# A six-chunk depthwise convolution on TensorE, roots as a power on GpSimd, weight splits on VectorE

## The chip, the cores and the metric

The kernel runs on one core of one Trainium2 chip. The metric is the device time of one execution in microseconds. Of the kernel before there are three timed runs (2513.06 to 2517.64 us, median 2514.32) and one profiled execution.

## The reference, cut to what matters

Two blocks in a row, on 256 tokens of 1024 features. The first block has two layers with a second stream, `ctx`, of 256 tokens beside `x`. Layer 0 of it is a half feed-forward, a conformer convolution and a half feed-forward; layer 1 has attention in the place of the convolution. Each part is preceded by an RMS norm that is scaled and shifted by a projection of a condition vector ("modulation"). The second block has a mixer of two kinds of attention with normed heads (AB), a gated feed-forward, a small gate, and then the same with a compressed and windowed attention (NSA).

```python
def rmsnorm(x, g):
    y = xf * lax.rsqrt(jnp.mean(xf * xf, axis=-1, keepdims=True) + NORM_EPS)
    return y.astype(x.dtype) * g
...
def conformer_conv(h, pw1_w, pw1_b, dw_w, dw_b, ln_g, ln_b, pw2_w, pw2_b):
    a = h @ pw1_w + pw1_b
    u, g = jnp.split(a, 2, axis=-1)
    u = u * jax.nn.sigmoid(g)
    u = lax.conv_general_dilated(u, dw_w[:, None, :], (1,), padding=[(15, 15)], ..., feature_group_count=D_MODEL) + dw_b
    mu = jnp.mean(uf, axis=-1, keepdims=True)
    var = jnp.mean(jnp.square(uf - mu), axis=-1, keepdims=True)
    u = (uf - mu) * lax.rsqrt(var + NORM_EPS) * ln_g + ln_b
    return jax.nn.silu(u) @ pw2_w + pw2_b
```

The depthwise convolution has 31 taps for each of the 1024 channels. Every `rsqrt` in both blocks is over one number per token (or per token and head).

## The kernel before

Features lie on the 128 partitions in eight chunks, tokens in the free dimension, 256 for each stream, so a product for both streams has 512 columns. Each weight product is three TensorE products (lines 337 to 339, or 360 to 362): the fp32 weight is split into a high part `wh` (ScalarE, L306) and a low rest `wl` (L308), in up to four or eight pieces for each loaded tile. `wl` is VectorE's, but in the two mixers of the second block `on_pool` gives the first pieces of a tile to GpSimd (ABP = 4, NSP = 2). Weights come in 1 MB loads on SP's DMA queue (L310), and the reductions of the modulation (L492, from `ada_t`) run on VectorE beside the work of each stage.

The order of the work on each engine is that of the code, in which a small planner, `Flow`, interleaves. It keeps a clock that each product group advances; `put(delay, f)` runs a step when that clock has passed the delay, `fill(gen, period)` draws steps of a generator at a period, and `until` runs steps until a condition holds. So an engine's order is fixed in advance, and each engine works its list in order.

A norm's root: squares are added chunk by chunk (ScalarE squares, GpSimd adds, L386 in `sq_add`), TensorE sums over partitions with a column of ones (L390), VectorE scales (L397) and takes the root in `rsqrt_small`: an integer first guess and three Newton rounds, ten VectorE instructions (L370, L373, L374, L376). Then `spread` puts the column on a diagonal (L406) and TensorE broadcasts it (L407).

The convolution: first the pointwise product for chunk pairs, gate and up, and the gating (L823, L824). Chunks 0 to 3 (`DIRECT`) are convolved tap by tap, 20 taps on VectorE (L841), 11 on ScalarE and GpSimd (L854, L855). Chunks 4 to 7 (`Taps`) go to DRAM (`gated`, L891) and come back with four copies (L897), each shifted by one token, on 32 channels' partitions, so that a 128x32 product (L907) applies four taps to 32 channels at once; its weights are diagonal matrices that GpSimd builds (L880). Each product is for one stream. The results are gathered with a shift by a pivot (L934) and their sums and squares added by GpSimd (L951, L955) for the LayerNorm's mean and variance (L964), then applied (L984, L985, L1040) and given to the second pointwise product, pw2.

The heads in the second block: `head_rms` reduces squares for each head (L1423), scales (L1425), takes the root and multiplies (L1437); TensorE transposes the result (L1463).

## Time and profile before

| | |
|---|---|
| median of three runs | 2514.32 us (2513.06 to 2517.64) |
| the profiled execution | 2520.06 us |
| its span, first to last instruction | 2518.2 us |
| mean granted TensorE clock, of 2.4 GHz | 0.970 |
| busy: TensorE / VectorE / ScalarE / GpSimd | 94% / 70% / 43% / 23% |
| DMA | 371.91 MB, 148 GB/s |

The span lies 1.86 us inside the execution's time. Every row below is from this one execution; times are microseconds from the span's start. "Idle before <- releaser" tells how long an engine had stood before an operation, and which operation on which engine ended that.

### The profile page before, as it was taken

How to read it: one execution, taken by the hardware profiler on the slowest of the kernel's cores; microseconds unless marked ns; L12 is line 12 of the kernel's file. 1: busy time of each engine (PE TensorE's matmuls, PEld its weight loads, DVE VectorE, ACT ScalarE, POOL GpSimd, SP SyncE). 2: the span in 40 equal slices, each digit the busy share in tenths (PEclk: the TensorE clock that was granted, in tenths of full speed). 3: DMA queues.
4: the chain of work that ended last, by engine and by line, in shares of the span. 5: the costliest groups of instructions: out<-in, count | busy, mean ns of one | idle time of the engine just before them, and what ended most of it. 6: DMA issues, size and time to landing. Idle time of an engine off the chain costs nothing. (4 is left out here: it accounts for less than half of the span.)

```text
span 2518.2 us, 40157 instructions
## 1 busy us (share of the span) xinstructions
PE 2360.3 (94%) x15397; PEld 2107.0 (84%) x15397; DVE 1754.9 (70%) x3816; ACT 1075.2 (43%) x2497; POOL 569.3 (23%) x595
## 2 busy tenths in 40 slices
...
GB/s 262 232 158 176 125 176 151 59 126 67 64 138 138 177 104 167 97 138 150 184 150 209 105 68 110 254 205 168 114 103 176 187 177 177 118 66 161 176 176 114
DMA packets 313149, 371.91 MB, mean 148 GB/s; under 512 B 9307, under 2 KB 298236, under 8 KB 305148
## 3 DMA queue, kind: packets, MB, share of 16 engines
...
## 5 line engine op out<-in xcount | busy, mean ns | idle before, releaser
L337 PE MATMUL ps<-a,wh 128*128 128x256 f32 (+2 forms) x4032 | 1310.7, 327 | 20.3 <-ACT wh L306 9.2
L339 PE MATMUL ps<-a,wl 128*128 128x256 f32 (+2 forms) x4032 | 1310.0, 325 | 6.5 <-DVE wl L308 6.5
L338 PE MATMUL ps<-a,wh 128*128 128x256 f32 (+2 forms) x4032 | 1311.7, 326 | 3.7 <-DVE a L1290 1.4
L306 ACT ACTIVATE wh<-stg 128x512 fp32r<-128x512 f32 (+1 forms) x1280 | 609.5, 539 | 598.9 <-PE ps L338 328.5
L337 PEld LDWEIGHTS ps<-a,wh 128*128 128x128 f32 x4032 | 771.3, 192 | 93.1 <-ACT wh L306 11.2
L339 PEld LDWEIGHTS ps<-a,wl 128*128 128x128 f32 x4032 | 774.5, 192 | 68.0 <-DVE wl L308 7.5
L338 PEld LDWEIGHTS ps<-a,wh 128*128 128x128 f32 x4032 | 775.5, 192 | 66.6 <-POOL a L553 2.0
L308 DVE TENSOR_TENSOR wl<-stg,wh 128x512 fp32r<-128x512 f32 (+1 forms) x1206 | 692.7, 626 | 162.9 <-ACT wh L306 157.2
L561 POOL TENSOR_TENSOR a<-t,a 128x256 fp32r<-128x256 f32 (+1 forms) x128 | 136.2, 1066 | 1338.5 <-ACT a L560 1286.5
L492 DVE CUSTOM_DVE_ANT_0 void<-stg,cb,vec 128x1024 f32<-128x1024 f32 x208 | 276.7, 1330 | 41.3 <-DMA stg<-ada_t 37.4
L560 ACT ACTIVATE a<-t 128x256 fp32r<-128x256 f32 (+1 forms) x152 | 76.5, 504 | 254.9 <-DVE t L621 176.3
L657 DVE SCALAR_TENSOR_TENSOR a<-ps,mv,a 128x256 f32<-128x256 f32 x232 | 101.4, 477 | 77.2 <-PE ps L339 77.1
L621 DVE TENSOR_TENSOR t<-t,ps 128x512 f32<-128x512 f32 x66 | 45.4, 687 | 151.6 <-PE ps L339 139.1
L386 POOL TENSOR_TENSOR acc<-acc,t 128x256 f32<-128x256 f32 x98 | 95.7, 977 | 205.0 <-ACT t L385 201.8
L361 PE MATMUL ps<-wl,a 128*128 128x256 f32 x384 | 112.2, 292 | 8.2 <-DVE wl L308 6.9
L360 PE MATMUL ps<-wh,a 128*128 128x256 f32 x384 | 112.7, 294 | 1.7 <-ACT wh L306 1.7
L308 POOL TENSOR_TENSOR wl<-stg,wh 128x512 fp32r<-128x512 f32 (+1 forms) x74 | 93.8, 1296 | 88.7 <-ACT wh L306 88.7
L362 PE MATMUL ps<-wh,a 128*128 128x256 f32 x384 | 111.3, 290 | 0.0
L620 ACT ACTIVATE t<-ps 128x512 f32<-128x512 f32 x66 | 39.0, 590 | 108.2 <-PE ps L339 108.2
L361 PEld LDWEIGHTS ps<-wl,a 128*128 128x128 f32 x384 | 76.7, 200 | 9.7 <-DVE wl L308 7.3
L360 PEld LDWEIGHTS ps<-wh,a 128*128 128x128 f32 x384 | 76.5, 199 | 2.7 <-ACT wh L306 1.9
L841 DVE SCALAR_TENSOR_TENSOR a<-a,vec,a 128x512 f32<-128x512 f32 x76 | 78.3, 1095 | 0.0
(310 smaller groups left out, 1957.0 us busy)
## 6 DMA issues: line engine op xcount, KB each, us to landing
...
```

Source lines behind the costliest of these rows:

```text
L306: nc.scalar.activation(wh[:, k], st[:, k], AF.Copy)
L308: e.tensor_tensor(wl[:, k], st[:, k], wh[:, k].bitcast(F32), ALU.subtract)
L337: nc.tensor.matmul(out, wh[:, k, js], h, start=(k == 0), stop=False)
L338: nc.tensor.matmul(out, wh[:, k, js], l, start=False, stop=False)
L339: nc.tensor.matmul(out, wl[:, k, js], h, start=False, stop=(k == n - 1))
L360: nc.tensor.matmul(out, h[:, ts], wh[:, k, :], start=(k == 0), stop=False)
L361: nc.tensor.matmul(out, h[:, ts], wl[:, k, :], start=False, stop=False)
L362: nc.tensor.matmul(out, l[:, ts], wh[:, k, :], start=False, stop=(k == n - 1))
L386: nc.gpsimd.tensor_tensor(acc, acc, t, ALU.add)
L492: nc.vector.tensor_tensor_reduce(self.void, st[:, i], self.cb[:, s], 1.0, V("ada_b", 72 * layer + v + i), ALU.mult, ALU.add, mv[layer][:, ...
L561: eng.tensor_tensor(l, src, h.bitcast(F32), ALU.subtract)
L657: nc.vector.scalar_tensor_tensor(x[s][:, m, :], o, g, x[s][:, m, :], ALU.mult, ALU.add)
```

## The change

Convolution: `DIRECT` falls from 4 to 2. The 31 taps of chunks 0 and 1 are all VectorE's, and accumulate in PSUM. Chunks 2 to 7 are tap products. For each, the gated chunk is written to DRAM as plain rows, 128 of 2072 bytes, with three zeros ahead of each stream's tokens, and read back by one DMA of 1.06 MB whose access pattern overlaps: 32 rows at a time, each four times, shifted by one. For this the channel order of the first pointwise weights, their bias and the tap weights is permuted on the host. Write and read-back are on ScalarE's DMA queue, at planned delays `OUT` and `BACK`. A tap product takes both streams (512 columns); for the last two chunks it takes one stream at a time. Tap weights are built one chunk at a time in a pool of three buffers that the modulation's broadcast condition (`cb`) and scratch (`void`) use too; `cb` is loaded anew behind the convolution (`sums.spread()`). The pivot comes from chunk 2.

Roots: `rsqrt_small` is one GpSimd `tensor_tensor` with the power -0.5. Two small scalings of `head_rms` go to GpSimd.

Splits: all `wl` are VectorE's; the odd chunks of a modulation are made as the even ones. Of the convolution's apply, the even chunks' splits are VectorE's now.

Sums: the last chunk's square isn't added by GpSimd, but summed by further products of one column.

```diff
-POOL_TAPS = 11
-DIRECT = 4
-SLICE = 3.5
+DIRECT = 2
+SLICE = 2.9
+LAG = 2
 ADA0 = 4.0
 ADA1 = 5.0
+OUT = 1.5
+BACK = 3.5
...
-PIVN = 1
-GQP = 0
-ABP = 4
-NSP = 2
...
+    mhalf = cp.tile([P, 16], F32, name="mhalf")
+    nc.vector.memset(mhalf, -0.5)
...
-            e = eng or (nc.gpsimd if i < share else nc.vector)
+            e = eng or nc.vector
...
     def rsqrt_small(v, out=None):
-        n = v.shape[1]
-        y = tiny()[:, :n]
-        nc.vector.tensor_scalar(y.bitcast(I32), v.bitcast(I32), -0.5, 1597463007.0, ALU.mult, ALU.add)
-        for i in range(3):
-            t = tiny()[:, :n]
-            nc.vector.scalar_tensor_tensor(t, y, -0.5, y, ALU.mult, ALU.mult)
-            nc.vector.tensor_tensor(t, t, v, ALU.mult)
-            z = out if (i == 2 and out is not None) else tiny()[:, :n]
-            nc.vector.scalar_tensor_tensor(z, t, 1.5, y, ALU.add, ALU.mult)
-            y = z
+
+        y = tiny()[:, :v.shape[1]] if out is None else out
+        nc.gpsimd.tensor_tensor(y, v, mhalf[:, :v.shape[1]], ALU.pow)
         return y
...
+    def sq_last(src, scale=1.0):
+
+        t = tmp()[:, :S]
+        nc.scalar.activation(t, src, AF.Square, scale=scale)
+        return t
...
+            for i, part in enumerate(parts):
+                nc.tensor.matmul(p[:, c0 + t:c0 + t + 1], part[:, t * P:(t + 1) * P], ones[:, 0:1],
+                                 start=(i == 0), stop=(i == len(parts) - 1))
...
+        def spread(self):
+
+            self.cb = [np_.tile([P, D], F32, name="w4", bufs=3) for _ in range(2)]
+            for s, t in enumerate(self.cb):
+                nc.sync.dma_start(t, a["cR"][s:s + 1].to_broadcast([P, D]))
+                nc.scalar.activation(t, t, AF.Silu)
+            self.void = np_.tile([P, D], F32, name="w4", bufs=3)
...
-            if c % 2 == 0:
-                nc.scalar.activation(h, t, AF.Identity, bias=sh)
-                nc.vector.scalar_tensor_tensor(l, t, sh, h.bitcast(F32), ALU.add, ALU.subtract)
-            else:
-                nc.scalar.activation(t, t, AF.Identity, bias=sh)
-                nc.scalar.activation(h, t, AF.Copy)
-                nc.gpsimd.tensor_tensor(l, t, h.bitcast(F32), ALU.subtract)
+            nc.scalar.activation(h, t, AF.Identity, bias=sh)
+            nc.vector.scalar_tensor_tensor(l, t, sh, h.bitcast(F32), ALU.add, ALU.subtract)
...
+    gated = tc.dram_tile([DC - DIRECT, 256 * SW + 3], F32, name="gated")
+    ups = [np_.tile([P, 2, SW], F32, name="up", bufs=2) for _ in range(2)]
+    for t in ups:
+        nc.gpsimd.memset(t[:, :, 0:3], 0.0)
+    nc.scalar.dma_start(gated[:, 256 * SW:], ups[0][0:DC - DIRECT, 0, 0:3])
+    npiv = tmp()
+    sums4 = np_.tile([P, 2, 2 * S], F32, name="w4", bufs=3)
...
-        nv = TAPS - POOL_TAPS
-        zs = [tmp().rearrange("p (s n) -> p s n", s=2) for _ in range(2)]
-        for k in range(max(nv, POOL_TAPS)):
-            for j in range(2 if k < nv else 0):
...
+        ds = [bank() for _ in range(2)]
+        for k in range(TAPS):
+            for j in range(2):
+                y, src, wk = two(ds[j]), padded[:, j, :, k:k + S], V("dw_k", j * TAPS + k)
+                if k == 0:
                     nc.vector.tensor_scalar(y, src, wk, None, ALU.mult)
                 else:
-                    for s in both:
-                        nc.vector.scalar_tensor_tensor(y[:, s], src[:, s], wk, convs[s].npiv, ALU.mult, ALU.add)
-            for j in range(2 if k < POOL_TAPS else 0):
-                c, up, z = m + j, padded[m // 2][:, j], zs[j]
-                src, wk = up[:, :, nv + k:nv + k + S], V("dw_k", c * TAPS + nv + k)
-                if k == 0:
-                    nc.gpsimd.tensor_scalar(z, src, wk, V("dw_b", c), ALU.mult, ALU.add)
-                else:
-                    t = tmp().rearrange("p (s n) -> p s n", s=2)
-                    nc.scalar.activation(t, src, AF.Identity, scale=wk)
-                    nc.gpsimd.tensor_tensor(z, z, t, ALU.add)
-            if k % 2 == 1:
-                yield True
+                    nc.vector.scalar_tensor_tensor(y, src, wk, y, ALU.mult, ALU.add)
+            yield True
...
+    def tap_weights(c):
+
+        t = np_.tile([P, 2 * 2 * S], F32, name="w4", bufs=3)
+        tap_w[c] = t.rearrange("p (n k) -> p n k", k=32)
+        for i in range(2):
             v = V("dw_w", 32 * (c - DIRECT) + 16 * i, 16).unsqueeze(2).to_broadcast([P, 16, 32])
-            nc.gpsimd.tensor_tensor(w, v, eye4.unsqueeze(1).to_broadcast([P, 16, 32]), ALU.mult)
-
-    def two_tap_weights(c, t):
-        for i in range(2):
-            tap_weights(c + i, [t[:, 2 * i], t[:, 2 * i + 1]])
-
-    class Taps:
-        def __init__(self, c, u, g):
-            self.c = c
-            up = tmp()
-            glu(c, u, g, up.rearrange("p (s n) -> p s n", s=2))
-            nc.sync.dma_start(gated[c].rearrange("p g n -> g p n"), up)
-            self.src = slot([P, 4, 2, SW])
-            for n in (0, S):
-                nc.gpsimd.memset(self.src[:, :, :, n:n + 3], 0.0)
-            gc = gated[c].rearrange("p g (s n) -> p (g s) n", s=2)
-            for i in range(4):
-                nc.sync.dma_start(self.src[32 * i:32 * i + 32, :, :, 3 - i:3 - i + S]
-                                  .rearrange("p g s n -> p (g s) n"), gc)
-
-        def products(self, s):
-            p = bank()[:, :S]
-            order = (3, 0, 1, 2, 4, 5, 6, 7)
-            for q in order:
-                lo, hi = max(0, 12 - 4 * q), min(S, S + 15 - 4 * q)
-                n = 4 * q - 12
-                for g in range(4):
-                    nc.tensor.matmul(p[32 * g:32 * g + 32, lo:hi], tap_w[self.c][q // 4][:, q % 4 * 4 + g, :],
-                                     self.src[:, g, s, lo + n:hi + n], start=(q == order[0]),
-                                     stop=(q == order[-1]), tile_position=(0, 32 * g))
-                flow.adv(0.5)
-            return p
+            nc.gpsimd.tensor_tensor(tap_w[c][:, 16 * i:16 * i + 16], v, eye4.unsqueeze(1).to_broadcast([P, 16, 32]),
+                                    ALU.mult)
...
+    def bounce(c, u, g):
+
+        up = ups[c % 2]
+        glu(c, u, g, up[:, :, 3:])
+        d = gated[c - DIRECT]
+
+        def back():
+            chunks[c] = slot([P, 4, 2, SW])
+            nc.scalar.dma_start(chunks[c].rearrange("p g s n -> p (g s n)"),
+                                bass.AP(tensor=d.tensor, offset=d.offset, ap=[[8 * SW, 32], [1, 4], [1, 8 * SW]]))
+
+        def out():
+            nc.scalar.dma_start(d[0:256 * SW].rearrange("(p n) -> p n", p=P), up.rearrange("p s n -> p (s n)"))
+            flow.put(BACK, back)
+
+        flow.put(OUT, out)
+
+    def products(c, streams):
+        p = bank()
+        order = (3, 0, 1, 2, 4, 5, 6, 7)
+        ss = slice(streams[0], streams[-1] + 1)
+        flow.until(lambda: c in chunks)
+        for q in order:
+            lo, hi = max(0, 12 - 4 * q), min(S, S + 15 - 4 * q)
+            n = 4 * q - 12
+            for g in range(4):
+                nc.tensor.matmul(two(p)[32 * g:32 * g + 32, ss, lo:hi], tap_w[c][:, 4 * q + g, :],
+                                 chunks[c][:, g, ss, lo + n:hi + n], start=(q == order[0]),
+                                 stop=(q == order[-1]), tile_position=(0, 32 * g))
+            flow.adv(0.43 * len(streams))
+        take(c, p, streams)
...
+        if c == DIRECT:
+            nc.scalar.activation(y, p, AF.Identity, bias=V("dw_b", c))
+            pv = bank()
+            nc.tensor.matmul(pv, ones, y, start=True, stop=True)
+            nc.scalar.activation(npiv, pv, AF.Copy, scale=-1.0 / P)
+            nc.vector.tensor_tensor(y, y, npiv, ALU.add)
+        else:
+            nc.vector.scalar_tensor_tensor(y, p[:, cols], V("dw_b", c), npiv[:, cols], ALU.add, ALU.add)
+        q = tmp()[:, cols]
+        nc.scalar.activation(q, y, AF.Square)
+        if c == DIRECT:
+            held.extend((y, q))
+        elif c == DC - 1:
+            for s in streams:
+                convs[s].last = (y, q)
+        else:
+            for i, new in enumerate((y, q)):
+                nc.gpsimd.tensor_tensor(sums4[:, i, cols], held.pop(0) if held else sums4[:, i, cols], new, ALU.add)
...
-                split(acts[c], t2, nc.gpsimd)
+                split(acts[c], t2, nc.vector if c % 2 == 0 else nc.gpsimd)
...
+                bounce(c, u, g)
+            if c == DIRECT - 1:
+                flow.fill(direct(), SLICE)
+                tap_weights(DIRECT)
+                tap_weights(DIRECT + 1)
+            if c - LAG >= DIRECT:
+                products(c - LAG, both)
+                if c < DC:
+                    tap_weights(c)
     ws = [wtile(pw2[:, i * 256:(i + 1) * 256], DC) for i in range(3)]
     ws.append(prepare(pw2[:, 768:1024], DC, 256, ap))
     flow.until(lambda: ended)
-    for c in (DC - 2, DC - 1):
-        taps(c, 0)
-    flow.until(lambda: len(ended) == DIRECT // 2)
-    taps(DC - 3, 1)
+    products(DC - 2, (0,))
+    products(DC - 1, (0,))
...
-    taps(DC - 2, 1)
-    taps(DC - 1, 1)
+    products(DC - 2, (1,))
+    products(DC - 1, (1,))
...
+    sums.spread()
...
-        nc.vector.tensor_scalar(e[:, 0:2], var, EPS, None, ALU.mult)
+        nc.gpsimd.tensor_scalar(e[:, 0:2], var, EPS, 0.0, ALU.mult, ALU.add)
         nc.vector.tensor_reduce(v, sq.rearrange("p (n d) -> p n d", d=64), AX.X, ALU.add)
         for t in range(2):
-            nc.vector.tensor_scalar(v[:, t * ng:(t + 1) * ng], v[:, t * ng:(t + 1) * ng], 1.0 / HD, e[:, t:t + 1],
+            nc.gpsimd.tensor_scalar(v[:, t * ng:(t + 1) * ng], v[:, t * ng:(t + 1) * ng], 1.0 / HD, e[:, t:t + 1],
                                     ALU.mult, ALU.add)
...
-    on_pool[0] = ABP
...
-    on_pool[0] = NSP
...
+def by_fours(v):
+
+    v = v.reshape(-1, 2, DC, 4, 32).copy()
+    v[:, :, DIRECT:] = v[:, :, DIRECT:].swapaxes(3, 4).reshape(-1, 2, DC - DIRECT, 4, 32)
+    return v.reshape(-1, 2 * D)
...
-    put("eye4", np.tile(np.eye(32), (4, 1)))
+    put("eye4", np.repeat(np.eye(32), 4, 0))
...
-    nc = bacc.Bacc("TRN2", target_bir_lowering=False, num_devices=1, dynamic_dma_scratch_size=2048)
+    nc = bacc.Bacc("TRN2", target_bir_lowering=False, num_devices=1, dynamic_dma_scratch_size=256)
```

VectorE ahead of the first mixer's heads, before. `tn` and `col` are columns of a few numbers, `t` the heads' values; the row with two `tn` inputs is a Newton step.

```order
L1423 TENSOR_REDUCE tn<-t_15310 128x8
L1383 TENSOR_TENSOR col<-col,tn 128x2
L1425 TENSOR_SCALAR tn<-tn 128x4 x2
L370 TENSOR_SCALAR tn<-tn 128x8
L373 SCALAR_TENSOR_TENSOR tn<-tn 128x8
L374 TENSOR_TENSOR tn<-tn 128x8
L376 SCALAR_TENSOR_TENSOR tn<-tn 128x8
...
L1437 TENSOR_TENSOR t_15309<-t_15130,tn 128x256 x2
L1423 TENSOR_REDUCE tn<-t_15338 128x8
```

Ten steps stand between the scaling L1425 and the product L1437: one L370, and L373, L374 and L376 three times. VectorE at the same place, after (L1387 and L1401 are L1423 and L1437 of before):

```order
L1387 TENSOR_REDUCE tn_14898<-t2_14896 128x8
L1347 TENSOR_TENSOR col_14889<-col_14882,tn_14887 128x2
L305 TENSOR_TENSOR wl_14923<-stg_14921,wh_14922 128x512
L1401 TENSOR_TENSOR t2_14895<-t2_14742,tn_14904 128x256 x2
L305 TENSOR_TENSOR wl_14923<-stg_14921,wh_14922 128x512
L1387 TENSOR_REDUCE tn_14911<-t2_14909 128x8
L305 TENSOR_TENSOR wl_14923<-stg_14921,wh_14922 128x512
L1401 TENSOR_TENSOR t2_14908<-t2_14743,tn_14917 128x256 x2
L305 TENSOR_TENSOR wl_14923<-stg_14921,wh_14922 128x512
```

The ten steps have left VectorE's list, and weight pieces (L305) that GpSimd had stand between the heads. GpSimd's list at this place, after; L367 is the power:

```order
L376 TENSOR_TENSOR t_14515<-t_14515,t_14707 128x256
L367 TENSOR_TENSOR col<-tn,mhalf 128x2
L367 TENSOR_TENSOR tn<-tn,mhalf 128x2
L1386 TENSOR_SCALAR tn<-col 128x2
L1389 TENSOR_SCALAR tn<-tn 128x4 x2
L367 TENSOR_TENSOR tn<-tn,mhalf 128x8
```

Where weight pieces stood, GpSimd now has for each head group its two scalings and the root.

GpSimd at the norm ahead of the convolution, after. `acc` is the sum of squares of stream 1, the first power (`col`) its root; `w` are tap weights (L866) and, at L924, the convolution's sums:

```order
L376 TENSOR_TENSOR acc<-acc,t_3096 128x256
L376 TENSOR_TENSOR acc<-acc,t_3100 128x256
L376 TENSOR_TENSOR acc<-acc,t_3104 128x256
L866 TENSOR_TENSOR w_3423<-vec,eye_3145 128x512 x2
L866 TENSOR_TENSOR w_3426<-vec,eye_3145 128x512 x2
L866 TENSOR_TENSOR w_3711<-vec,eye_3145 128x512 x2
L367 TENSOR_TENSOR col<-col,mhalf 128x2
L924 TENSOR_TENSOR w_3156<-a_3143 128x512
```

Six tap-weight pieces stand between the last add of a square and the root of the same stream; before, no tap weights were built until the convolution had begun, and the root was VectorE's.

SP's queue in the convolution, before, in which `stg` are weight loads:

```order
L891 DMA gated<-t_3782 4x32x512
L897 DMA a_3787<-gated 32x8x256 x4
L891 DMA gated<-t_3850 4x32x512
L310 DMA stg<-ffn_wi 128x8x256
L897 DMA a_3855<-gated 32x8x256 x4
```

Write and copies of a chunk stood between weight loads. ScalarE there, after; L833 is a gate's sigmoid, L303 a `wh` piece, L908 and L911 belong to the pivot, L916 squares:

```order
L833 ACTIVATE t_3661<-ps,vec 128x512
L881 DMA gated<-up 128x518
L877 DMA a_3698<-gated 128x1x2072
L908 ACTIVATE a_3143<-ps,vec 128x512
L911 ACTIVATE t_3155<-ps 128x512
L916 ACTIVATE t_3709<-a_3143 128x512
L303 ACTIVATE wh<-stg 128x512
L833 ACTIVATE t_3768<-ps,vec 128x512
L303 ACTIVATE wh<-stg 128x512 x6
L881 DMA gated<-up 128x518
L303 ACTIVATE wh<-stg 128x512
L877 DMA a_3805<-gated 128x1x2072
```

The write and the read-back of a chunk have moved among ScalarE's own work, the read-back behind the write.

## Rows read from the trace of the kernel before

**Rows 1.** Page, part 1: busy us, share of the span, instructions.
```profile
PE 2360.3 (94%) x15397; PEld 2107.0 (84%) x15397; DVE 1754.9 (70%) x3816; ACT 1075.2 (43%) x2497; POOL 569.3 (23%) x595
```

**Rows 2.** TensorE's waits: total us, times, longest.
```profile
PE ps L907 <- DMA a<-gated: 22.3, 2, 21.8
PE ps L407 <- DVE t L406: 19.0, 9, 5.2
PE ps L1463 <- DVE t L1437: 18.3, 3, 16.3
PE ps L964 <- POOL acc L955: 15.2, 2, 15.0
PE ps L390 <- POOL acc L386: 9.7, 5, 3.1
```

**Rows 3.** Stretches: us, busy PE PEld DVE ACT POOL, clock, DMA share, GB/s.
```profile
545.00:614.00 69.00, 27.63 (x357) 17.47 (x349) 55.51 (x76) 22.40 (x43) 49.68 (x43) 0.69 0.49 111
1778.00:1795.00 17.00, 0.67 (x3) 0.45 (x3) 16.22 (x34) 6.16 (x13) 11.48 (x10) 0.63 0.44 142
...
2095.00:2235.00 140.00, 120.32 (x924) 114.31 (x923) 111.95 (x358) 83.07 (x227) 51.32 (x70) 0.93 0.39 114
```

**Rows 4.** Timeline of TensorE in the convolution: start, us, operation, idle before.
```profile
450.02 0.40 PE L337 MATMUL ps<-a,wh 128*128 128x512 f32 x1
450.25 0.40 PE L338 MATMUL ps<-a,wh 128*128 128x512 f32 x1
...
486.57 0.79 PE L337 MATMUL ps<-a,wh 128*128 128x512 f32 x1 [9.17 <-ACT wh L306]
...
494.26 0.79 PE L339 MATMUL ps<-a,wl 128*128 128x512 f32 x1 [6.47 <-DVE wl L308]
...
535.19 10.32 PE L907 MATMUL ps<-a,a 128*32 128x256 f32 x192
...
567.28 5.18 PE L907 MATMUL ps<-a,a 128*32 128x256 f32 x64 [21.77 <-DMA a<-gated]
...
594.93 0.58 PE L964 MATMUL ps<-ones,acc 128*128 128x1 f32 x2 [15.00 <-POOL acc L955]
...
610.86 1.46 PE L407 MATMUL ps<-t,ones 128*128 128x128 f32 x8 [2.24 <-DVE t L406]
613.98 1.01 PE L337 MATMUL ps<-a,wh 128*128 128x256 f32 x3 [1.66 <-ACT a L560]
```

**Rows 5.** VectorE: its direct taps (timeline), and a PSUM operand (page, part 5).
```profile
472.97 19.57 DVE L841 SCALAR_TENSOR_TENSOR a<-a,vec,a 128x512 f32<-128x512 f32 x12
...
500.09 8.03 DVE L841 SCALAR_TENSOR_TENSOR a<-a,vec,a 128x512 f32<-128x512 f32 x12
...
L657 DVE SCALAR_TENSOR_TENSOR a<-ps,mv,a 128x256 f32<-128x256 f32 x232 | 101.4, 477 | 77.2 <-PE ps L339 77.1
```

**Rows 6.** Timeline of SP's queue: a chunk's write and its read-back.
```profile
508.80 0.69 SPq L891 DMA_DIRECT2D gated<-t  x1
514.80 2.59 SPq L897 DMA_DIRECT2D a<-gated  x4
```

**Rows 7.** Timeline: VectorE's modulation and root steps, and GpSimd's pieces.
```profile
424.39 1.75 DVE L492 CUSTOM_DVE_ANT_0 void<-stg,cb,vec 128x1024 f32<-128x1024 f32 x1
...
681.67 0.17 DVE L370 TENSOR_SCALAR tn<-col 128x2 int32<-128x2 int32 x1
...
683.43 0.16 DVE L376 SCALAR_TENSOR_TENSOR col<-tn 128x2 f32<-128x2 f32 x1
...
1786.39 1.19 DVE L376 SCALAR_TENSOR_TENSOR tn<-tn 128x8 f32<-128x8 f32 x1
...
1785.06 8.60 POOL L308 TENSOR_TENSOR wl<-stg,wh 128x512 fp32r<-128x512 f32 x7 [3.08 <-ACT wh L306]
```

**Rows 8.** GpSimd's groups: operation xcount | busy us, mean ns | idle before.
```profile
L1485 POOL TENSOR_SCALAR a<-a,tn 128x128 f32<-128x128 f32 x32 | 11.9, 372 | 47.8 <-DVE tn L1523 26.2 <-DVE tn L1859 17.1 <-ACT a L1144 2.9
...
L951 POOL TENSOR_TENSOR acc<-t,t 128x256 f32<-128x256 f32 x1 | 10.0, 9964 | 0.0
```

166 lines of the change are left out of this document (49 added, 117 removed).

## The prediction

> **What bounds the kernel now.** I read the busy times first, then the list of what TensorE waited for, then the table by stage, then the timeline at the long waits. TensorE is busy for 94% of the span, VectorE for 70% and GpSimd for 23% [rows 1]. So whatever this change gains must come out of the remaining 6% (about 153 us, the sum of all of TensorE's idle stretches), out of the slow clock that follows a long idle stretch, and out of the TensorE work itself, of which the change takes none away and adds some. The waits say where that idle time lies [rows 2]: 22.3 us behind the DMA that brings the gated conv input back, 15.2 us behind GpSimd's adds L955, 19.0 us in nine waits for the spread of a norm's root (L406), 9.7 us in five waits for the sum of squares (L386), 18.3 us behind the scaled heads (L1437). The table by stage gives the clock beside it [rows 3]: between 545 and 614 us TensorE is busy for 27.63 of 69 us and was granted 0.69 of its 2.4 GHz; between 1778 and 1795 us it is busy for 0.67 of 17 at 0.63; between 2095 and 2235 us it idles 19.7 us. So the conv is the largest place, then the attention's first heads, then the roots.
>
> **The conv, 450 to 614 us.** The six weight groups of 512 columns begin at 450.02 us and the second pointwise product begins at 613.98 [rows 4]: 164.0 us. Three kinds of wait lie in it: 9.17 and 6.47 us for weight pieces, because VectorE had twelve taps queued ahead of them; 21.77 us for the read-back; 15.00 us for GpSimd's last sums [rows 4]. The taps ahead of the pieces took 19.57 us for twelve with GpSimd adding beside them, and 8.03 us for twelve without [rows 5]: two engines that halve each other.
>
> After the change I count TensorE's own work, all at the 2.4 GHz level.
> - Six chunks, u and g, 24 products each: 288 at 0.23 us (from 450.02 to 450.25 is one step [rows 4]) make 66.2 us. This is as before.
> - Tap products. Of before, the stretch at 535.19 us holds three chunk-streams (one chunk of one stream, 32 products, two records each: 192 records) in 10.32 us [rows 4], so 3.44 us for one. Now twelve chunk-streams run instead of eight (six chunks by two): 41.3 us. Two streams in one product save instructions, not columns, so I take no gain for it.
> - The pivot (a copy out of PSUM and one product of ones): 1.5 us. The sums of stream 0: 1.5 us. From the last tap product to pw2, the spread and the first apply: 613.98 minus 610.86, 3.1 us [rows 4].
>
> Sum 113.6 us, against 164.0. What could still stand in the way: VectorE's work in that stretch is 62 direct taps at 0.67 [rows 5], 20 us of weight pieces and about 10 us of gates and takes, 71 us of 113. The accumulator of the direct taps moves to PSUM, where an operation of half the width keeps a mean of 0.477 us over the whole span, with GpSimd busy or not (L657 [rows 5]), so the halving should go; if not, the 62 take 101 us and the stretch is VectorE's. GpSimd's work is twelve tap-weight pieces and fourteen adds, at 1.23 us each (seven operations of this size in 8.60 us [rows 7]) to 1.6, 32 to 42 us: no bound. The round trip through DRAM: the write is issued at 508.80 and the read-back could be issued at 514.80 [rows 6], 6.0 us, then some 5 us for the transfer. Five of six round trips have two chunks of other work (21 us and more) to hide in; the last has only the products of chunk 6, about 7 us and what is left of the direct part. I allow 2 us there. The two DMAs now stand on ScalarE's queue, and the read-back waits there for the write to land: behind it ScalarE's next weight pieces are held. The order shows one or two pieces between the two, and the pieces behind are those of a group later. I allow 2 us, bounds 0 and 4 times 6.0 us. Conv: 113.6 + 4 = 117.6, a gain of **46.4 us** (bounds 25 and 52).
>
> **The roots.** A root is now ten VectorE steps, the first at 681.67 and the last at 683.43 us, 1.92 us with its end [rows 7], where nothing disturbs it. With GpSimd on weight pieces (from 1785.06) a step takes 1.19 instead of 0.16 us [rows 7]. After, it is one GpSimd `pow` on 2 to 8 columns. No row shows a pow. The nearest rows are GpSimd's 128x128 scaling at 0.372 us [rows 8] and its 128x512 operation at 1.23 [rows 7]; I take 0.4 us plus the two hand-overs between the engines, 0.6 to 0.8 us in all, because two columns are nearer to the first. For the ends I keep 0.2 (the fixed part of the first) and 1.5.
>
> At the norms: of the 19.0 us for L406, 2.24 lie in the conv [rows 4] and some 2 in the opening; 14.8 us belong to the four norms. I take 1.2 us off each of the seven and 3 us more at the last (5.2 us long because the ten steps stood between other work): 10 us of 14.8. Each of the five waits for L386 loses one GpSimd add, about 1 us: 5 us of 9.7 [rows 2]. About 2 us of slow clock go with them. Against this stands a new wait. The order puts six tap-weight pieces on GpSimd ahead of stream 1's root at the norm in front of the conv. They can start only when the modulation's reductions have left the same buffers. The reduction that the new order has last ended at 426.1 us (424.39 and 1.75 [rows 7]); six pieces of 1.23 us, 7.4 us, bring the root to about 434 us. TensorE will be there at about 430. I put 4 us against it (bounds 0 and 8). Norms: **-13 us** (bounds -20 and -2).
>
> **The first heads, 1754 to 1800 us.** TensorE stands 16.33 us for L1437, since the roots of the heads crawl beside GpSimd's pieces [rows 2, 3, 7]. After, GpSimd has no pieces; VectorE takes them. In the order 16 pieces stand among the four heads' steps: 16 x 0.67 = 11 us (by the undisturbed operation of the same size in [rows 5]), plus the reductions and scalings of four heads, 6 us, plus small steps: 18 us from 1754.7, so done at about 1773. TensorE comes for them at 1778. The gap closes, a 1.7 us gap behind it too, and about 2 us of slow clock. If pow costs 1.5 us the four of them still fit. **-20 us** (bounds -10 and -23).
>
> **The second attention, 2095 to 2235 us.** The same two edits apply, but the waits there are many and small, 19.7 us of idle in all [rows 3], and a part of them for weight pieces. VectorE loses some 25 us of root steps and gets 32 pieces, 20 us: about even, so a piece may still come late. I take 7 us of the 19.7 (bounds 2 and 13).
>
> **The other edits.** The last square goes into the sum by one more product of one column instead of a GpSimd add (counted above). ScalarE and GpSimd no longer make the odd chunks of a modulation; VectorE does it at 0.5 us each, in stretches where TensorE has ten times that queued: nothing, and 1 us per norm if the cover is gone. The reload of cR behind the conv puts a 1 MB load on SP and one ScalarE operation ahead of the first apply; this is inside the 2 us above.
>
> **What the skill says.** The Trainium skill, GPSIMD Engine Reference, section 3.1, holds that "use DVE for elementwise" stays the rule, and section 2.1 that the first call of a freshly loaded GpSimd kernel pays about 6 us more without an instruction of its own. The first part does not decide here, since one operation replaces ten. By the second, if pow needs such a load, the estimate would be 6 us worse, 2434. No row here shows such a load. The order has an extra instruction of no named kind on GpSimd ahead of the first pow, in the opening, where TensorE waits for a root.
>
> **The sum.** 46.4 + 13 + 20 + 7 = 86.4 us. The profiled execution took 2520.06 us, 5.7 more than the median of the three runs, so it would go to 2433.7 and the median, 2514.32, to **2428**.
>
> **Rivals.**
> 1. The forecast, 2405 to 2450: chance 0.60.
> 2. *ScalarE's queue becomes the wait.* In each of the last four round trips ScalarE stands for the landing, 6.0 us [rows 6], and the weight pieces behind it reach TensorE late: 24 us less, and some clock lost again: about 2454. For it: the queue is in order, and weight pieces do stand behind the read-back. Against: ScalarE is busy for 22.40 of the 69 us [rows 3]. Chance 0.15.
> 3. *Pow costs 1.5 to 4 us.* Then the norms gain nothing or lose 10 us and the second attention gains nothing: 2514.3 - 46.4 - 10 + 5 = 2463, up to about 2515 at the far end. Chance 0.12.
> 4. *Slower: pow is the bound.* TensorE waits for a root at 12 places (nine L406, three L1437 [rows 2]). GpSimd's longest simple operation took 9.96 us [rows 8], with nothing in the row to say why. At this price 12 x (9.96 - 1.92) = 96 us come on top, while conv, pieces and adds give 58: 2552. It decides from 58 / 12 + 1.92 = 6.8 us. Against: GpSimd's time grows with columns in every other row. Chance 0.06.
> 5. *More:* the second attention's and the norms' waits go entirely and the conv's allowance is not needed: 52 + 20 + 23 + 15 = 110, 2404 and below. Chance 0.07.
>
> **How the numbers follow.** About 0.2% (5 us) is what a measurement of this kernel can tell from no change. Cases 1, 2 and 5 are faster; of case 3 all but 0.04 (split between same and slower); case 4 is slower. With 0.01 of case 2 as same: faster 0.90, same 0.03, slower 0.07. The range takes the forecast's own 2405 to 2450, rival 2 and the near half of rival 3, and its lower end reaches a little into rival 5: 2402 to 2465.
>
> **What would show it.** Right: no wait for the read-back above 3 us in TensorE's list, pw2's first product at about 565 us in the span, the 16 us wait before the first head's transposes gone, pow under 0.5 us, at least 0.9 of the clock in the conv. A wait of some 4 us for the root of stream 1 ahead of the conv is expected. Wrong: waits for ScalarE's weight pieces in the conv (rival 2), pow in microseconds (3, 4), direct taps still at 1.6 us beside GpSimd (then the conv lasts 30 us longer).

## The result, and the profile after

The changed kernel takes **2457.78 us** (median of 4 runs, 2456.79 to 2461.86) against 2513.69 for the kernel before, measured beside it (median of 4, 2511.81 to 2517.64). The ratio is 0.9779, with a 95% interval of 0.9762 to 0.9796: 56 us faster, inside the range, 30 us above the 2428 of the forecast. The profiled execution took 2457.87 us, with a span of 2456.1.

The busy times and the list of what TensorE waited for, after (columns as in [rows 1, 2]; L404/L405 are L406/L407 of before, L387 is L390, L895 the tap products, L940 the convolution's sums, L1401 is L1437, L1105 a copy out of PSUM):

```profile
PE 2366.3 (96%) x15459; PEld 2100.7 (86%) x15459; DVE 1636.6 (67%) x3527; ACT 1039.4 (42%) x2414; POOL 406.4 (17%) x479
```

```profile
PE ps L405 <- DVE t L404: 13.4, 7, 5.8
...
PE ps L387 <- POOL acc L376: 7.4, 4, 2.5
PE ps L1459 <- DVE a L1105: 6.6, 2, 5.3
...
PE ps L940 <- POOL w L924: 4.0, 1, 4.0
PE ps L1101 <- DVE tn L1840: 3.7, 1, 3.7
PE ps L1101 <- DVE a L1105: 3.6, 2, 3.4
...
PE ps L895 <- DMA a<-gated: 1.4, 1, 1.4
```

Of the five waits of [rows 2], the 22.3 us for the read-back are 1.4, the 15.2 for GpSimd's sums 4.0, the 18.3 for the scaled heads are one wait of 0.7 us far down the list, the 19.0 for a root's spread are 13.4 and the 9.7 for the squares 7.4. All idle time of TensorE fell from 153.3 to 85.2 us. New are 5.3 us behind a copy out of PSUM in the first mixer (L1459 for L1105; 0.8 before) and 3.7 us behind a scaling step of the second attention (L1840). The 3.6 us of L1101 for L1105 stood there before too, at 3.7.

To see where the time went I compare the start of the same TensorE instruction in both traces, the spread of a norm's root (L407 before, L405 after), 17 times in the program. The difference grows like this (us, after minus before):

| up to | start before | start after | difference | gain of the part | forecast |
|---|---|---|---|---|---|
| norm ahead of the conv, stream 1 | 434.92 | 429.95 | -5.0 | norms: 5.0 | norms: 13, all of them |
| conv's root | 610.86 | 568.25 | -42.6 | conv: 37.6 | conv: 46.4 |
| norm behind pw2, stream 1 | 684.64 | 648.32 | -36.3 | **6.3 given back** | nothing |
| cross-attention | 1557.62 | 1511.56 | -46.1 | norms: 9.8 | (in the 13) |
| behind the first mixer | 1896.00 | 1837.50 | -58.5 | 12.4 | 20 |
| end | 2497.82 | 2435.73 | -62.1 | 3.6 | 7 |

The table's sum is 6 us more than the medians differ, since the profiled execution of before (2520.06) lay above its median and the one of after does not. Where these 6 us lie is worked out behind the experiments.

The convolution in stretches, after (columns as in [rows 3]), and its timeline on TensorE:

```profile
445.00:545.00 100.00, 98.67 (x620) 64.94 (x618) 73.04 (x111) 30.60 (x53) 12.84 (x11) 1.00 0.48 164
545.00:571.00 26.00, 18.83 (x216) 11.79 (x216) 7.73 (x19) 4.97 (x9) 10.97 (x11) 0.80 0.25 83
```

```profile
429.95 1.22 PE L405 MATMUL ps<-t,ones 128*128 128x128 f32 x4 [5.77 <-DVE t L404]
...
446.06 0.40 PE L335 MATMUL ps<-a,wh 128*128 128x512 f32 x1
...
545.84 3.58 PE L895 MATMUL ps<-a,w 128*32 128x256 f32 x64 [1.36 <-DMA a<-gated]
553.37 0.59 PE L940 MATMUL ps<-ones,w 128*128 128x1 f32 x2 [3.95 <-POOL w L924]
...
568.25 1.16 PE L405 MATMUL ps<-t,ones 128*128 128x128 f32 x8 [0.80 <-DVE t L404]
571.21 0.73 PE L334 MATMUL ps<-a,wh 128*128 128x256 f32 x4 [1.80 <-ACT a L561]
```

For 100 us TensorE is busy for 98.67 at a granted clock of 1.00: the holes of [rows 4] are gone. From 446.06 to 571.21 the convolution takes 125.2 us where it took 164.0. The last 26 us still hold waits of 1.36, 3.95 and 1.80 us, at a clock of 0.80.

GpSimd's groups for L367, the power, after (line, operation, names, shapes, count; then busy us and mean ns of one):

```profile
L367 POOL TENSOR_TENSOR tn<-tn,mhalf 128x8 f32<-128x8 f32 x14 | 23.0, 1641 | 1.2
L367 POOL TENSOR_TENSOR col<-col,mhalf 128x2 f32<-128x2 f32 x14 | 11.9, 854 | 56.0 <-DVE col L395 56.0
...
L367 POOL TENSOR_TENSOR tn<-tn,mhalf 128x4 f32<-128x4 f32 x1 | 1.0, 1024 | 14.1 <-DVE tn L705 14.1
...
L367 POOL TENSOR_TENSOR tn<-tn,mhalf 128x2 f32<-128x2 f32 x1 | 0.7, 698 | 0.7 <-DVE tn L1344 0.7
L367 POOL TENSOR_TENSOR tn<-tn,mhalf 128x1 f32<-128x1 f32 x1 | 0.6, 562 | 6.8 <-DVE tn L1726 6.8
```

The power costs 0.70 us on two columns in most calls and 1.64 on eight. The prediction had one price for both, 0.4.

### The profile page after: what moved, and what is told of

The parts are those of the page before. It is cut to its first block, busy times and chain, and to the rows that moved or that the text cites. A ratio compares the mean times of both kernels' runs of the same rounds, so it can differ in the third digit from the quotient of the medians.

```text
span 2456.1 us, 39668 instructions
## 1 busy us (share of the span) xinstructions
PE 2366.3 (96%) x15459; PEld 2100.7 (86%) x15459; DVE 1636.6 (67%) x3527; ACT 1039.4 (42%) x2414; POOL 406.4 (17%) x479
## 5 line engine op out<-in xcount | busy, mean ns | idle before, releaser
L303 ACT ACTIVATE wh<-stg 128x512 fp32r<-128x512 f32 (+1 forms) x1280 | 609.1, 539 | 591.0 <-PE ps L335 319.6
L305 DVE TENSOR_TENSOR wl<-stg,wh 128x512 fp32r<-128x512 f32 (+1 forms) x1276 | 719.6, 617 | 170.2 <-ACT wh L303 165.4
L562 POOL TENSOR_TENSOR a<-t,a 128x256 fp32r<-128x256 f32 (+1 forms) x120 | 129.6, 1081 | 1373.2 <-ACT a L561 1256.7
L495 DVE CUSTOM_DVE_ANT_0 w<-stg,w,vec 128x1024 f32<-128x1024 f32 x208 | 274.4, 1319 | 43.4 <-DMA stg<-ada_t 39.5
L376 POOL TENSOR_TENSOR acc<-acc,t 128x256 f32<-128x256 f32 x84 | 82.3, 979 | 212.2 <-ACT t L375 209.4
L357 PEld LDWEIGHTS ps<-wh,a 128*128 128x128 f32 x384 | 75.6, 197 | 2.8 <-ACT wh L303 1.9
L359 PEld LDWEIGHTS ps<-wh,a 128*128 128x128 f32 x384 | 75.4, 196 | 0.0
L553 ACT ACTIVATE a<-t,mv 128x256 fp32r<-128x256 f32 x80 | 35.7, 501 | 80.3 <-DVE t L549 80.2
```

What stands on the lines that cost most here:

```text
L303: nc.scalar.activation(wh[:, k], st[:, k], AF.Copy)
L305: e.tensor_tensor(wl[:, k], st[:, k], wh[:, k].bitcast(F32), ALU.subtract)
L357: nc.tensor.matmul(out, h[:, ts], wh[:, k, :], start=(k == 0), stop=False)
L359: nc.tensor.matmul(out, l[:, ts], wh[:, k, :], start=False, stop=(k == n - 1))
L376: nc.gpsimd.tensor_tensor(acc, acc, t, ALU.add)
L495: nc.vector.tensor_tensor_reduce(self.void, st[:, i], self.cb[s], 1.0, V("ada_b", 72 * layer + v + i), ALU.mult, ALU.add, mv[layer][:, v + ...
```

## The experiments

The first theory was: the conv and the norms do what was forecast, and the missing 30 us lie in the heads' roots on GpSimd, in the sums' wait, in the tap weights ahead of the root, and in the modulation's reductions that have come behind the conv. The rivals: ScalarE's queue holds the weight pieces (rival 2 of the prediction), or the edits take the same time twice. Eight kernels undo or change a part of the kernel after, two put a part alone into the kernel before, two join what helped. All ratios are against the kernel before on the same chip. Its median was 2513.69 to 2515.36 us on the chips used, so I read nothing into a microsecond or two between two variants.

### The heads' roots back on VectorE

```diff
+    def rsqrt_newton(v, out=None):
...
-        nc.gpsimd.tensor_scalar(e[:, 0:2], var, EPS, 0.0, ALU.mult, ALU.add)
+        nc.vector.tensor_scalar(e[:, 0:2], var, EPS, None, ALU.mult)
...
-            nc.gpsimd.tensor_scalar(v[:, t * ng:(t + 1) * ng], ...
+            nc.vector.tensor_scalar(v[:, t * ng:(t + 1) * ng], ...
...
-        r = rsqrt_small(v)
+        r = rsqrt_newton(v)
```

> The changed kernel, with the roots of the heads (8 columns) and their two small scalings back on VectorE as the ten Newton steps; all other roots stay a power on GpSimd. Theory: in the changed kernel the power takes 1.64 us for 8 columns and 0.70 us for 2, and with the two scalings ahead of it and softmax scalings queued on the same engine VectorE stands 2.2 to 4.3 us for each head group, with copies that TensorE needs behind it. Undisturbed, ten steps take 2.0 us of VectorE and wait for nobody. So TensorE's gaps of 5.3 us in the first mixer and 3.4, 3.5 and 3.7 us in the second shrink: 5 to 10 us less than the changed kernel (2457.8), 2448 to 2453. Rival: VectorE's own queue is the bound there (it has all weight pieces now), so that ten steps cost what the wait cost: 2455 to 2460.

Measured: 2439.87 us (2436.5 to 2442.08), ratio 0.9702 [0.9688, 0.9717]: 18 us faster than after, where I had expected 5 to 10. Up to the cross-attention its spreads start within 0.3 us of those of after; then the difference to before reaches -69.5 behind the first mixer (after -58.5) and -83.5 at the end (after -62.1): 11 us in the first mixer, 10 in the second. The trace of after shows why. GpSimd, then VectorE, then TensorE, at a head group of the first mixer (L1389 is a scaling of the heads, L1449/L1450 scale softmax rows, L1459 takes what L1105 copied):

```profile
1753.22 0.48 POOL L1450 TENSOR_SCALAR a<-a,tn 128x256 f32<-128x256 f32 x1
1753.81 0.64 POOL L1389 TENSOR_SCALAR tn<-tn 128x4 f32<-128x4 f32 x2
1754.53 1.64 POOL L367 TENSOR_TENSOR tn<-tn,mhalf 128x8 f32<-128x8 f32 x1
```

```profile
1756.20 0.42 DVE L1401 TENSOR_TENSOR t<-t,tn 128x256 f32<-128x256 f32 x1 [3.65 <-POOL tn L367]
...
1756.94 1.98 DVE L305 TENSOR_TENSOR wl<-stg,wh 128x512 fp32r<-128x512 f32 x3
1758.84 1.47 DVE L1105 COPY a<-ps 128x384 f32<-128x384 f32 x3
```

```profile
1759.53 1.13 PE L1459 MATMUL ps<-a,a 128*64 128x256 f32 x4 [5.33 <-DVE a L1105]
```

Read it downwards. The two scalings and the power stand behind softmax scalings in GpSimd's queue and end at 1756.17. VectorE stands 3.65 us at L1401 for them, and behind L1401 in its queue stand three weight pieces and the PSUM copies for which TensorE waits 5.33 us. In the variant VectorE fills the same time with weight pieces between the ten steps, each step 0.16 or 0.17 us:

```profile
1714.11 0.17 DVE L373 TENSOR_SCALAR tn<-tn 128x8 int32<-128x8 int32 x1
1714.18 0.69 DVE L305 TENSOR_TENSOR wl<-stg,wh 128x512 fp32r<-128x512 f32 x1
1714.78 0.17 DVE L376 SCALAR_TENSOR_TENSOR tn<-tn 128x8 f32<-128x8 f32 x1
```

and the wait of 5.33 us is gone. So with no weight pieces on GpSimd, scalings and ten steps in VectorE's own queue (1.7 us for the steps) beat scalings and an eight-column power in GpSimd's. The run moves both back, so it does not show how the 18 us divide between the power and the scalings. Here these 18 us agree with the Trainium skill, GPSIMD Engine Reference, section 3.1 ("use DVE for elementwise"), which I had set aside in the prediction; the next run, at two columns, speaks against it.

### All roots back on VectorE

In the same way, but with the ten steps in `rsqrt_small` itself, for the norms too.

> The changed kernel with every root back as ten VectorE steps. Theory: the heads gain as in the run with only them back (5 to 10 us), and the norms lose what the power of two columns saves there (0.7 us on GpSimd against 1.9 us on VectorE, about 1 us at each of some eight norms, and the long wait at the norm ahead of the convolution, where the power stands behind tap weights, goes): within 4 us of that run. Rival: the power is what gave the norms their gain, 10 us and more: 2460 or above.

Measured: 2461.74 us, 0.9794 [0.9777, 0.981]: 22 us slower than the variant above. So the powers of the norms, with the other small roots, are worth 22 us, and my expectation was wrong. The list of waits shows it for the root's spread, first here, then with the norms' powers (lines shifted by 6 between the two):

```profile
PE ps L412 <- DVE t L411: 21.6, 10, 5.9
```

```profile
PE ps L418 <- DVE t L417: 13.1, 6, 5.8
```

At a norm the root has two columns: 0.70 us against 1.92 for the ten steps [rows 7]. Of the 22 us the list shows 8.5; by the ledger 14.6 had come up by the cross-attention, 6.3 more in the first mixer and 4.3 in the second (25 in the two traces, 22 by the medians). Why a norm gains more than its list of waits shows I did not separate.

### The weight pieces back on GpSimd

```diff
+    on_pool = [0]
...
-            e = eng or nc.vector
+            e = eng or (nc.gpsimd if i < share else nc.vector)
...
+    on_pool[0] = 4
...
+    on_pool[0] = 2
```

> The changed kernel with GpSimd's share of the weight pieces put back in the two mixers (4 and 2 of a tile's pieces, as before); the roots stay powers. Theory: the 16 us gap ahead of the first head's transposes came from GpSimd's pieces, not from where the root is computed: with powers queued behind pieces of 1.3 us each the gap comes back, 10 to 25 us more than the changed kernel. Rival: the gap came from the ten steps on VectorE and stays closed with a power: within 4 us of 2457.8.

Measured: 2473.08 us, 0.9837 [0.9822, 0.9852]: 15 us slower than after, as expected. The wait in front of the first heads does not come back as one (16.33 us before); in the trace of TensorE it returns in parts:

```profile
1732.40 1.75 PE L1430 MATMUL ps<-ident,t 128*128 128x128 f32 x12 [2.87 <-DVE t L1404]
...
1744.97 0.80 PE L1486 MATMUL ps<-a,a 64*128 64x128 f32 x4 [7.96 <-DVE a L1432]
...
1802.13 1.13 PE L1462 MATMUL ps<-a,a 128*64 128x256 f32 x4 [7.27 <-DVE a L1108]
```

### The convolution without the roots and without the pieces

Both of the last two edits in the kernel after: what is left of the change is the convolution, the last square and the splits of the modulation and of the convolution's apply. The heads' scalings are on VectorE here too.

> The changed convolution (with the sums of the last square by products and the shared buffers), but all roots as ten VectorE steps and GpSimd's share of the weight pieces as before. Theory: the convolution with what it costs behind it is worth 32 to 38 us: 2476 to 2482. Rival, as forecast: 46 us and more, 2468 or less. If roots and pieces help one another only together, the sum of the single steps falls short of the whole change.

Measured: 2486.71 us, 0.9898 [0.9878, 0.9918]: 28 us faster than before, 4 to 10 less than expected. In the first mixer the old wait is there as in [rows 2]:

```profile
1761.34 2.95 PE L1437 MATMUL ps<-ident,t 128*128 128x128 f32 x12 [15.66 <-DVE t L1411]
```

### The kernel before without weight pieces on GpSimd

```diff
-ABP = 4
-NSP = 2
+ABP = 0
+NSP = 0
```

> The kernel before with one edit: no weight pieces on GpSimd in the two mixers (4 and 2 become 0). Theory: with roots on VectorE in both, the runs with and without GpSimd's pieces on the changed convolution differ by 25 us, so the edit alone gives 20 to 28 us: 2487 to 2495. Rival: the gap of 16.3 us needs the roots moved too, and VectorE's added pieces cost what they free: 2505 or more.

Measured: 2487.02 us, 0.9886 [0.9872, 0.9899]: 28 us faster, the upper end of what I expected. The wait of 16.3 us falls to

```profile
PE ps L1463 <- DVE t L1437: 6.6, 2, 4.9
```

### The kernel before with the power for all its roots

`rsqrt_small` of after in the kernel before, the two scalings of the heads left on VectorE.

> The kernel before with one edit: the root as a power on GpSimd everywhere (the heads' small scalings stay on VectorE, GpSimd keeps its pieces). Theory: two columns take 0.70 us and gain at the norms, 12 to 16 us; at the heads eight columns take 1.64 us and stand behind pieces of 1.3 us, and give some of it back: 2498 to 2508. Rival: behind the pieces the heads lose more than the norms gain: 2512 or more.

Measured: 2483.34 us, 0.9873 [0.986, 0.9887]: 32 us faster, more than I expected. By the ledger 24 us come at the norms and 8 in the first mixer, where the old wait of 16.3 us is down to two of 1.88 and 1.08 us though the pieces are still on GpSimd (a new one, of 5.68 us for a PSUM copy, comes at 1821.11):

```profile
1756.73 0.33 PE L1458 MATMUL ps<-ident,t 128*128 128x128 f32 x1 [1.88 <-DVE t L1432]
1758.14 2.61 PE L1458 MATMUL ps<-ident,t 128*128 128x128 f32 x11 [1.08 <-DVE t L1432]
```

At the first heads the wait shrinks because, in the kernel before, 12 of the 30 Newton steps ahead of it took about 1.2 us beside GpSimd's pieces (one of them in [rows 7]; the other 18 took 0.17), and the power takes 1.64 us once:

```profile
1744.07 1.64 POOL L372 TENSOR_TENSOR tn<-tn,mhalf 128x8 f32<-128x8 f32 x1 [0.24 <-DVE tn L1420]
1745.67 7.90 POOL L310 TENSOR_TENSOR wl<-stg,wh 128x512 fp32r<-128x512 f32 x6
```

Whether the eight-column powers win here is not shown. The 8 us hold the mixer's small roots too, which gave 6.3 us there in the two runs above, and in the second attention this kernel gains nothing (403.2 us for the stretch, 403.0 before).

**What follows from these six.** Alone in the kernel before, the three parts give 28 (conv), 28 (no pieces) and 32 us (power): 88, close to the forecast 86. Together they give 56. Conv and pieces nearly add: the kernel with both and no power is at 2461.74, 53 us below before. The power then adds only 4: plus 22 at the norms and other small roots, minus 18 at the heads.

Two things are in this loss. The wait of 16.3 us was counted by two edits, and either of them closes most of it. And the changed kernel takes the heads' scalings to GpSimd with the power, which the run with the power alone did not. Their price can be read from the time between spreads, in the first mixer (cross-attention to behind the mixer) and from there to behind the second attention:

| kernel | first mixer | to behind the second attention |
|---|---|---|
| before | 338.4 | 403.0 |
| convolution alone | 338.3 | 403.4 |
| before with power, scalings on VectorE | 330.5 | 403.2 |
| after with pieces on GpSimd, scalings on GpSimd | 339.3 | 406.6 |

The convolution moves these two stretches by less than half a microsecond, so the last two rows differ in them by the scalings: some 12 us, beside the pieces. Without the pieces no run has the scalings or the power by themselves.

### The reductions behind pw2

```diff
+    late = tiny()
+    nc.vector.tensor_scalar(late[:, 0:1], x[1][:, 0, 0:1], 0.0, None, ALU.mult)
-    sums.spread()
+    sums.spread(late[:, 0:1])
...
+                    nc.scalar.activation(t, t, AF.Silu, bias=late)
```

The zero in `late` depends on the first chunk of x that pw2 writes for stream 1, so that the modulation's condition, and with it the reductions L495, come behind pw2.

> The changed kernel, with the reload of cR's activation made to depend on the second pointwise product's first result for stream 1, so that the modulation's next reductions can't start inside that product. Theory: the shared buffers push eight reductions of 1.27 us (10 us of VectorE) out of the convolution and in between the apply steps of pw2, where TensorE then waits 1.4, 0.7 and 3.1 us and some tenths and the lead of 42.6 us shrinks to 36.3 by the next norm. Without them: 4 to 7 us less than the changed kernel (2457.8), 2451 to 2454. Rival: the apply steps themselves (two VectorE, two ScalarE operations and a split for each chunk) are the pace there, or the reductions are missed later: within 3 us of 2457.8 or above.

Measured: 2448.40 us, 0.9736 [0.972, 0.9753]: 9 us faster than after. In after, eight reductions of 1.27 us stand between the steps of pw2's apply (L960, L961) on VectorE, two of them here:

```profile
574.70 0.41 DVE L960 TENSOR_TENSOR t<-a,ps 128x256 f32<-128x256 f32 x1
575.10 1.27 DVE L495 CUSTOM_DVE_ANT_0 w<-stg,w,vec 128x1024 f32<-128x1024 f32 x1
...
576.64 0.41 DVE L961 TENSOR_TENSOR t<-t,ps 128x256 f32<-128x256 f32 x1
577.04 1.28 DVE L495 CUSTOM_DVE_ANT_0 w<-stg,w,vec 128x1024 f32<-128x1024 f32 x1
```

Before, none stood there, and with the edit none does. With the edit the norm behind pw2 starts 47.1 us before that of before, in after 36.3: the 6.3 us of the ledger that were given back are not given back any more.

### The tap weights behind the root

```diff
+                zero = tiny()
+                nc.gpsimd.tensor_scalar(zero[:, 0:1], mod.cols[1][:, 0:1], 0.0, 0.0, ALU.mult, ALU.add)
+                nc.gpsimd.tensor_scalar(eye4, eye4, 1.0, zero[:, 0:1], ALU.mult, ALU.add)
```

> The changed kernel, with the tap weights' identity made to depend on stream 1's root ahead of the convolution, so that the six pieces stand behind the power on GpSimd. Theory: the 5.8 us wait for that root is the six pieces in front of it and falls below 3 us, with 0.5 to 1 us of slow clock: 3 to 5 us less than the changed kernel. Rival: the root is late because its sum of squares is (a 2 us wait stood there before too), so that nothing moves: within 2 us.

Measured: 2449.99 us, 0.9733 [0.9719, 0.9748]: 8 us faster than after. GpSimd in after had done the six tap-weight pieces ahead of the root of stream 1:

```profile
420.50 8.42 POOL L866 TENSOR_TENSOR w<-vec,eye 128x512 f32<-128x512 f32 x6 [1.83 <-DVE mv L495]
428.88 0.70 POOL L367 TENSOR_TENSOR col<-col,mhalf 128x2 f32<-128x2 f32 x1
```

With the edit, no wait over 1.2 us is left at this spread, and it starts at 422.77 in place of 429.95. Of these 7.2 us 2.8 are there already at the spread of stream 0, ahead of the edit; 4.4 belong to the wait. So of the 8 us by the medians the trace shows 4.4 at this place; the 2.8 are not the edit's, for with the same edit in the four repairs below the spread of stream 0 starts at 407.17, as in after (407.27).

### The direct part planned earlier

```diff
-SLICE = 2.9
+SLICE = 2.3
```

> The changed kernel with the planner's period for the direct taps at 2.3 instead of 2.9. By the order this leaves VectorE's list as it is, and moves ScalarE's squares of the two direct chunks ahead of the last weight pieces and the last read-back, and GpSimd's adds of them ahead of chunk 7's tap weights. Theory: the 4.0 us wait for GpSimd's sums comes from adds that bunch behind those late squares; it falls below 1.5 us and a part of the slow clock (0.80 over 26 us) goes with it: 3 to 6 us less than the changed kernel. Rival: the wait is for the adds of chunk 6 alone, which come last anyway: within 2 us.

Measured: 2452.65 us, 0.975 [0.9731, 0.9768]: 5 us faster than after by the medians, but the four runs lie between 2447.77 and 2458.36, so the size is uncertain. In the traces the conv's root comes 3.8 us earlier. In after, GpSimd stood 13.40 us for a buffer of the last tap weights (L866), with the direct chunks' sums (L924) behind it in its queue:

```profile
541.28 2.51 POOL L866 TENSOR_TENSOR w<-vec,eye 128x512 f32<-128x512 f32 x2 [13.40 <-PE ps L895]
543.75 3.40 POOL L924 TENSOR_TENSOR w<-w,a 128x512 f32<-128x512 f32 x2
```

Planned earlier, the direct sums run ahead of L866, and TensorE does not wait for them:

```profile
531.39 3.43 POOL L924 TENSOR_TENSOR w<-w,t 128x512 f32<-128x512 f32 x2
542.14 2.06 POOL L866 TENSOR_TENSOR w<-vec,eye 128x512 f32<-128x512 f32 x2 [7.33 <-PE ps L895]
```

The next thing is late instead, the last chunk's round trip:

```profile
548.80 5.26 PE L895 MATMUL ps<-a,w 128*32 128x256 f32 x64 [3.40 <-DMA a<-gated]
554.00 0.38 PE L940 MATMUL ps<-ones,w 128*128 128x1 f32 x2
```

### The round trip on SP's queue

```diff
-            nc.scalar.dma_start(chunks[c].rearrange(...
+            nc.sync.dma_start(chunks[c].rearrange(...
...
-            nc.scalar.dma_start(d[0:256 * SW].rearrange(...
+            nc.sync.dma_start(d[0:256 * SW].rearrange(...
```

> The changed kernel with the write and the read-back of each chunk on SP's queue, among the weight loads, in place of ScalarE's. Theory: ScalarE's waits for the landings (it stands up to 7 us ahead of a sigmoid) cost TensorE almost nothing in the changed kernel, 1.4 us in all; on SP the loads of the next weights stand behind each landing instead, so nothing is won: 2456 to 2466. Rival (the forecast's second case): ScalarE's blocked queue is what made the convolution 8 us longer than forecast; then it is 4 us or more faster, below 2454.

Measured: 2457.95 us, 0.9772 [0.9759, 0.9786]: the time of after. ScalarE does stand in after behind the last chunk's landing,

```profile
540.63 1.15 ACT L303 ACTIVATE a<-stg 128x512 fp32r<-128x512 f32 x2 [4.31 <-DMA gated<-up]
```

and no wait of TensorE for a weight piece stands in the convolution. With the round trip on SP the waits for the sums and for the read-back are 3.7 and 1.2 us, in after 4.0 and 1.4. Rival 2 of the prediction falls; that its 2454 us is the nearest number is luck.

### The four repairs together

The heads' roots on VectorE, the reductions, the tap weights and the earlier plan.

> The changed kernel with the roots of the heads on VectorE, the reductions behind pw2, the tap weights behind the root and the direct part planned earlier. Theory: the waits are in different stages, so the single gains add up: 18 us for the heads (measured) and 4, 4 and 4 for the others (expected), 2426 to 2432. Rival: they share slack, and 2434 to 2440 is left, as with the heads alone.

Measured: 2417.68 us (2415.66 to 2418.96), 0.9609 [0.9595, 0.9623]: 40 us below after. Alone the four gave 18, 9, 8 and 5, which is 40 too. The trace shows them one behind the other: against after, this run gains 5.3 us at the norm ahead of the conv, 6.2 in the conv, 5.7 behind pw2 and 21.2 in the two mixers. These four waits are independent.

### The repairs, with the last two squares summed by products

```diff
-            if m < DC - 1:
+            if m < DC - 2:
...
-                self.last[s] = sq_last(x[s][:, m, :])
+                self.last.setdefault(s, []).append(sq_last(x[s][:, m, :]))
...
-            _, self.cols[s] = rcol([self.accs[s], self.last[s]])
+            _, self.cols[s] = rcol([self.accs[s]] + self.last[s])
```

> The four repairs (2417.7), and at the modulated norms the last two chunks' squares, not one, summed by products of one column in place of a GpSimd add. Theory: TensorE still waits 1.7, 2.3 and 2.5 us for GpSimd's last add at three norms; one add less on that chain takes about 1 us off each: 2 to 4 us less, 2414 to 2416, hardly more than a measurement tells apart. Rival: the wait is for the last square itself: within 1 us.

Measured: 2409.40 us (2407.83 to 2414.41), 0.9586 [0.9572, 0.9599]: 8 us below the four repairs, more than expected, and the fastest of all: 48 us below after. Its TensorE waits for GpSimd's squares (`acc`) and for the roots:

```profile
PE ps L418 <- DVE t L417: 8.0, 5, 4.1
...
PE ps L400 <- POOL acc L389: 3.3, 2, 1.8
```

against 7.3 us in four for the squares with the four repairs alone. The list gives 4 of the 8 us; where the others lie I did not separate.

## Why the prediction was right, and where it was off

The direction and the range held, 0.90 was given to faster (the cases as listed add up to 0.89), and the waits at the two largest places went as described. From -86.4 to -62.1 us in the trace 24 us are missing; another 6 lie between trace and median.

- **Conv: 46.4 forecast, 38.8 from start to pw2.** The count of products was right: TensorE's 100 us at full clock went as added up, and two streams in one product indeed saved no time. The direct taps with their accumulator in PSUM ran at 8.0 us for twelve, as the fast case of [rows 5], but only 3 of 60 had GpSimd beside them, so this run hardly tests the argument about PSUM. The trace of before does: at L657, 15 of the 232 operations with a PSUM operand ran beside GpSimd and took 0.47 us like the others, while 10 of the 16 that read SBUF in its place did and took 0.79 instead of 0.48. Of the two allowances of 2 us, that for the last round trip was right (1.36), and that for ScalarE's queue was not needed (the run with SP's queue). What failed is the step "GpSimd's work is ... 32 to 42 us: no bound". I compared sums of work and not the queue's order: GpSimd stood 13.40 us at L866 with the sums behind it. That is 3.95 us of wait; the last 26 us went at a clock of 0.80, of which I did not separate this wait's part. Planning the direct part earlier gave some 5 us by the medians, 3.8 of them in the conv by its trace.
- **The reload of cR: "inside the 2 us above" forecast, 6.3 us lost.** I costed the load and one ScalarE operation. What moved with it were eight reductions of 1.27 us, since condition and scratch now use the tap weights' buffers and can't be there during the convolution. The order of VectorE would have shown them between pw2's apply steps. The experiment with the reductions behind pw2 gave 9 us.
- **Norms: 13 forecast, 14.8 by the ledger.** The sum is near, but not term by term, so some of it is luck. The terms that I named for the roots' spreads add up to 11.4, not the 10 I wrote. The squares were to lose 5 us of 9.7, and the list shows 2.3 (7.4 are left). The lines of the waits for spreads and squares shrank by 7.9 us together, against 14.8 in the ledger, and why a norm gains more than its waits stays open. The new wait at stream 1 came as forecast: the tap weights kept the root until 429.58 (forecast 434), and TensorE waited 5.77 where I had taken 4. That experiment gave 8 us by the medians, 4.4 of them at this wait in its trace.
- **First heads: 20 forecast, 12.4 measured. Second attention: 7 forecast, 3.6 measured.** The 16.3 us wait went, as forecast. Two terms failed. One is the size of the power: "0.4 us plus the two hand-overs", one price for 2 to 8 columns because two are nearer to the first row. At eight columns it is 1.64, in a queue with softmax scalings. The other is the heads' two scalings ahead of it, 0.64 to 0.93 us together and once 2.3, whose move to GpSimd I had given no price. "If pow costs 1.5 us the four of them still fit" was true of the first heads; it passed over the later ones, where VectorE stands at L1401 and the PSUM copies queue behind it. I had not named what is queued behind the instruction that got the new wait. With the heads' roots and scalings back on VectorE both places together give 18 us more; by the trace of that variant the first mixer gains 23.4 us and the second 14.0, past both terms of the forecast (20 and 7).
- **The profile's offset.** I carried over that the profiled execution of before lay 5.7 us above its median. That of after lies on its own (2457.87 and 2457.78): 6 us of the miss.
- **Rivals.** The third (power at 1.5 to 4 us, 2463) had the price for eight columns and not for two, so its loss at the norms did not come: there and at the other small roots the power gains 22 us. The fourth took its 10 us from an operation whose length was that one execution's (below); it was far off.
- **A rule that did not show.** That the first call of a freshly loaded GpSimd kernel pays about 6 us more is said by the Trainium skill, GPSIMD Engine Reference, section 2.1. No such time is seen here: the first power, in the opening, took 1.02 us on four columns, which fits the other sizes, and the first spread starts 0.9 us earlier than before. But GpSimd had stood idle for 14.1 us ahead of it, in which a load could have gone unseen, so this does not decide it.

Most of the offset can be placed. The kernel before without GpSimd's pieces is the same program up to the first mixer, and its profiled execution lay on its median. There the norm ahead of the conv comes at 433.25 us, the conv's root at 605.98 and the cross-attention at 1552.57 (before: 434.92, 610.86, 1557.62). So 1.7 of the 6 us lie ahead of the conv and 3.2 in it, where one GpSimd operation took 9.96 us in the trace of before [rows 8] and 1.19 in the other:

```profile
523.84 1.19 POOL L951 TENSOR_TENSOR acc<-t,t 128x256 f32<-128x256 f32 x1
```

Against that trace the ledger's conv is 34.4 us instead of 37.6 and its norms 13.7 instead of 14.8.

What stays open: how the heads' 18 us divide between power and scalings, why the norms gain more than their waits, and where four of the last edit's 8 us lie.
